# A max-pool-and-subtract kernel: loads and stores in one DMA queue in a fixed order, 4 MB tiles, no ScalarE

## The chip, the cores and the metric

The kernel runs on one core of one Trainium2 chip. The metric is the device time of one execution in microseconds. The profile's "span" runs from the first to the last of the program's own instructions and is 1.5 to 2.3 us shorter than the time. Executions of a kernel are timed several times; those called "fast" are within 1.5% of the fastest of the same kernel. A result counts as faster or slower only beyond 2%; a smaller difference is still told from noise by its 95% interval. Data move between memory and the core in DMAs; 16 DMA engines share each of them, and every engine takes its share as a row of packets. VectorE, ScalarE and GpSimd compute; SyncE and ScalarE issue DMAs here. In the views of the profile these engines are DVE, ACT, POOL and SP, with a q added where the engine only waits or issues.

## The reference

The input is 8 x 64 images of 256 x 256 float32. Each 8 x 8 window's maximum is subtracted from all 64 elements of the window.

```python
x_r = x.reshape(B, C, oH, pH, oW, pW)            # pH = pW = 8
pooled = x_r.max(axis=(3, 5))
upsampled = np.repeat(np.repeat(pooled, pH, axis=2), pW, axis=3)
return (x - upsampled).astype(np.float32)
```

134.2 MB come in and 134.2 MB go out. Eight image lines, 2048 floats or 8 KB, hold 32 whole windows; this is "a row" below. A tile holds R rows per partition, contiguous in memory for a partition.

## The kernel before

Two rows per partition make a tile of 2 MB, 64 tiles in all, in eight buffers. SyncE issues the loads and ScalarE the stores, so there are two DMA queues. A scheduler orders the instructions.

```python
R = 2
data_pool = ctx.enter_context(tc.tile_pool(name="data_pool", bufs=8))
...
for i in range(ntiles):
    dat = data_pool.tile([P, R, row_len], mybir.dt.float32, name="dat")
    nc.sync.dma_start(out=dat..., in_=src)                  # L42, queue 1
    for r in range(R):
        nc.vector.tensor_reduce(out=pooled[:, r], in_=in_v, # L49, max of each window
                                axis=XY, op=max)
    nc.scalar.activation(out=rep, in_=pooled broadcast 8x, func=Copy)   # L56
    for r in range(R):
        nc.vector.tensor_tensor(out=dat_v, in0=dat_v,       # L64
                                in1=rep[:, r] broadcast over 8 lines, op=subtract)
    nc.scalar.dma_start(out=dst, in_=dat...)                # L74, queue 10
```

(Arguments shortened.)

## Time and profile before

| | before |
|---|---|
| time, median | 631.79 us (631.71 to 631.91) |
| span of the profiled execution | 630.3 us |
| DMA rate from 100 to 580 us | 431 GB/s |
| VectorE busy | 564.7 us |

Lines of the page: busy time of the engines, then the 40 slices of the span (busy tenths, GB/s of DMA), the DMA queues, the chain that ended last by engine, and the three costly groups of instructions (busy us, mean ns of one, idle time before them and its releaser).

```profile
DVE 564.7 (90%) x256; ACT 39.5 (6%) x65; POOL 0.2 (0%) x4
DMA  9999999999999999999999999999999999999997
GB/s 361 418 433 433 432 431 432 428 431 433 431 428 433 432 432 433 433 431 432 431 429 431 433 432 428 432 432 431 433 433 431 433 429 429 431 433 433 431 405 334
q1 hardware_dynamic: 9216, 134.22, 50.0%
q10 hardware_dynamic: 9216, 134.22, 49.8%
DMA 81%; DVE 16%; issue 1%; DVEq 0%; ACT 0%; SPq 0%; ACTq 0%
L49 DVE TENSOR_REDUCE pooled<-dat 128x32 f32<-128x2048 f32 x128 | 285.0, 2276 | 57.6 <-DMA dat<-in_x_dram 57.6
L64 DVE TENSOR_TENSOR dat<-dat,rep 128x2048 f32<-128x2048 f32 x128 | 283.9, 2282 | 0.8 <-ACT rep L56 0.8
L56 ACT ACTIVATE rep<-pooled 128x512 f32<-128x512 f32 x64 | 38.2, 624 | 578.4 <-DMA dat<-in_x_dram 408.2
```

The DMA engines are the limit: the row of nines is full, and the rate hardly moves. VectorE is not far behind but waits for loads. The slices at both ends are the only ones clearly lower.

Lines of the timeline of the kernel before at its end (start us, duration us, instruction), then its windows view (window, its length, busy us of VectorE, ScalarE and GpSimd, clock, DMA share, GB/s).

```profile
606.80 8.88 DVE L64 TENSOR_TENSOR dat<-dat,rep 128x2048 f32<-128x2048 f32 x4
...
618.64 4.49 DVE L64 TENSOR_TENSOR dat<-dat,rep 128x2048 f32<-128x2048 f32 x2 [0.76 <-ACT rep L56]
623.17 0.34 ACTq L74 DMA_DIRECT2D out_dram<-dat  x1
```

```profile
620.00:622.00 2.00, 2.00 (x2) 0.00 (x0) 0.00 (x0) 1.00 0.92 393
622.00:624.00 2.00, 1.13 (x1) 0.00 (x0) 0.00 (x0) 1.00 0.02 8
624.00:626.00 2.00, 0.00 (x0) 0.00 (x0) 0.00 (x0) 1.00 1.21 508
626.00:628.00 2.00, 0.00 (x0) 0.00 (x0) 0.00 (x0) 1.00 0.96 410
628.00:630.00 2.00, 0.00 (x0) 0.00 (x0) 0.00 (x0) 1.00 0.31 131
```

The queues run dry at the end because the last store waits for VectorE: 8 GB/s from 622 to 624 us, and the store is issued only at 623.17. (The view counts a packet whole in the window in which it starts, so a short window can show more than the steady rate, as the 508 here.)

### The profile page before, as it was taken

Reading aid. Unit: us, or ns where it says so; the run is one execution under the profiler, and the core shown is the slowest. Engines: PE = TensorE matmul, PEld = TensorE weight load, DVE = VectorE, ACT = ScalarE, POOL = GpSimd, SP = SyncE. Lnnn points to the kernel's source line nnn. Section 1 sums busy time; section 2 is a strip of 40 time slices with the busy share of each in tenths; the row PEclk is TensorE's granted clock in tenths of the full one; section 3 lists DMA queues with packets and bytes.
Section 4 is the critical chain, followed back from the end, with each engine's and each line's share of the span. In section 5 each row is a group of like instructions: output and inputs, shape, how many; then the busy total and the mean of one; then the engine's idle time right before and its main releaser. Section 6 shows DMA issues by size and latency. Waiting matters only on the chain.

```text
span 630.3 us, 730 instructions
## 1 busy us (share of the span) xinstructions
DVE 564.7 (90%) x256; ACT 39.5 (6%) x65; POOL 0.2 (0%) x4
## 2 busy tenths in 40 slices
DVE  4999999889889889889889898898998988988985
ACT  1000010010000000000001001001001001001000
POOL 0000000000000000000000000000000000000000
DMA  9999999999999999999999999999999999999997
GB/s 361 418 433 433 432 431 432 428 431 433 431 428 433 432 432 433 433 431 432 431 429 431 433 432 428 432 432 431 433 433 431 433 429 429 431 433 433 431 405 334
DMA packets 18437, 268.48 MB, mean 426 GB/s; under 512 B 2048, under 2 KB 2048, under 8 KB 2048
## 3 DMA queue, kind: packets, MB, share of 16 engines
q1 hardware_dynamic: 9216, 134.22, 50.0%
q10 hardware_dynamic: 9216, 134.22, 49.8%
q14 instruction: 5, 0.04, 0.0%
HBM read 134.22 MB, written 134.22 MB: 426 GB/s over the span
## 4 chain that ended last, share of the span: by engine, by line
DMA 81%; DVE 16%; issue 1%; DVEq 0%; ACT 0%; SPq 0%; ACTq 0%
DMA dat<-in_x_dram 49%; DMA out_dram<-dat 32%; DVE dat L64 9%; DVE pooled L49 7%; DVEq L100 0%; ACT rep L56 0%; SPq L42 0%; ACTq L74 0%; DVEq L64 0%; ACTq L56 0%
## 5 line engine op out<-in xcount | busy, mean ns | idle before, releaser
L49 DVE TENSOR_REDUCE pooled<-dat 128x32 f32<-128x2048 f32 x128 | 285.0, 2276 | 57.6 <-DMA dat<-in_x_dram 57.6
L64 DVE TENSOR_TENSOR dat<-dat,rep 128x2048 f32<-128x2048 f32 x128 | 283.9, 2282 | 0.8 <-ACT rep L56 0.8
L56 ACT ACTIVATE rep<-pooled 128x512 f32<-128x512 f32 x64 | 38.2, 624 | 578.4 <-DMA dat<-in_x_dram 408.2
L56 ACT ACT_TABLE_LOAD x1 | 1.3, 1283 | 0.7 <-PEq L89 0.7
L89 POOL MEMSET const-uint8-127<- 128x1 uint8 x1 | 0.1, 103 | 0.0
L89 POOL MEMSET const-bfloat16-1.0<- 128x1 bf16 x1 | 0.1, 102 | 0.0
L89 POOL MEMSET const-float32-0.0<- 128x1 f32 x1 | 0.1, 99 | 0.2 <-issue 0.2
L89 POOL MEMSET const-float32-1.0<- 128x1 f32 x1 | 0.1, 99 | 0.0
## 6 DMA issues: line engine op xcount, KB each, us to landing
dat<-in_x_dram SPq DMA_DIRECT2D x64, 2048.0 KB, 29.6
out_dram<-dat ACTq DMA_DIRECT2D x64, 2048.0 KB, 19.0
```

What stands on the lines that cost most here:

```text
L49: nc.vector.tensor_reduce(out=pooled[:, r], in_=in_v, axis=mybir.AxisListType.XY, op=mybir.AluOpType.max,)
L56: nc.scalar.activation(out=rep.rearrange("p r (ow pw) -> p (r ow) pw", pw=pW), in_=pooled.rearrange("p r ow -> p (r ow)").to_broadcast([P, ...
L64: nc.vector.tensor_tensor(out=dat_v, in0=dat_v, in1=rep[:, r].unsqueeze(1).to_broadcast([P, pH, W]), op=mybir.AluOpType.subtract,)
L89: nc = _bacc.Bacc("TRN2", target_bir_lowering=False, num_devices=1)
```

## The change

The intent: fewer and larger transfers (32 KB per partition), a fixed order in which a store never stands in front of a load that is needed sooner, small pieces at both ends, and no ScalarE in the computation. Core of the diff, with cuts and comments added:

```diff
-    R = 2
-    data_pool = ctx.enter_context(tc.tile_pool(name="data_pool", bufs=8))
+TILES = [[2, 2]] + [[4]] * 30 + [[2, 1, 1]]      # rows per piece, pieces per tile
+BUFS = 6
+LEAD = 3
...
-        nc.scalar.activation(out=rep..., in_=pooled..., func=Copy)
-            nc.vector.tensor_tensor(..., in1=rep[:, r]..., op=subtract)
+            nc.vector.tensor_reduce(out=tops, in_=all R rows, ...)      # L50
+        for r in range(R):
+            nc.vector.tensor_tensor(                                     # L57
+                out=wins[:, r], in0=wins[:, r],
+                in1=tops[:, r].unsqueeze(1).unsqueeze(3).to_broadcast([P, pH, oW, pW]),
+                op=mybir.AluOpType.subtract)
...
+    ctx.enter_context(tc.manual_schedule())
+    waiting = []
+    def store():
+        dst, part = waiting.pop(0)
+        nc.sync.dma_start(out=dst, in_=part)                             # L69
...
+        for R in pieces:
+            nc.sync.dma_start(out=part, in_=src)                         # L83
+            if len(waiting) == LEAD:
+                store()
+            pool_and_subtract(part, tops, R)
+            waiting.append((dst, part))
+    while waiting:
+        store()
```

After four loads SyncE's queue reads: store, load, store, load, each of 4 MB.

More of the change, by code (lines that the diff above doesn't have):

```diff
@@ L7 @@
 from concourse._compat import with_exitstack
+F32 = mybir.dt.float32
+ROW = 2048
+TILES = [[2, 2]] + [[4]] * 30 + [[2, 1, 1]]
+BUFS = 6
+LEAD = 3
 @with_exitstack
@@ L21, with pool_and_subtract @@
     pH = pW = 8
-    oH, oW = H // pH, W // pW
+    oW = W // pW
     x_rows = x.rearrange("b c (oh ph) w -> (b c oh) (ph w)", ph=pH)
     out_rows = out.rearrange("b c (oh ph) w -> (b c oh) (ph w)", ph=pH)
-    n_rows = x_rows.shape[0]
-    row_len = x_rows.shape[1]
-    R = 2
-    rows_per_tile = P * R
-    ntiles = n_rows // rows_per_tile
-    assert n_rows % rows_per_tile == 0
-    data_pool = ctx.enter_context(tc.tile_pool(name="data_pool", bufs=8))
-    small_pool = ctx.enter_context(tc.tile_pool(name="small_pool", bufs=4))
-    for i in range(ntiles):
-        dat = data_pool.tile([P, R, row_len], mybir.dt.float32, name="dat")
-        src = x_rows[i * rows_per_tile : (i + 1) * rows_per_tile].rearrange(
-            "(p r) d -> p (r d)", r=R
-        )
-        nc.sync.dma_start(out=dat.rearrange("p r d -> p (r d)"), in_=src)
-        pooled = small_pool.tile([P, R, oW], mybir.dt.float32, name="pooled")
-        rep = small_pool.tile([P, R, W], mybir.dt.float32, name="rep")
-        for r in range(R):
-            in_v = dat[:, r].rearrange("p (ph ow pw) -> p ow ph pw", ph=pH, ow=oW, pw=pW)
+    assert sum(map(sum, TILES)) * P == x_rows.shape[0]
+    size = max(map(sum, TILES))
+    data = ctx.enter_context(tc.tile_pool(name="data", bufs=BUFS))
+    small = ctx.enter_context(tc.tile_pool(name="small", bufs=BUFS))
+    def pool_and_subtract(dat, tops, R):
+        wins = dat.rearrange("p (r ph ow pw) -> p r ph ow pw", r=R, ph=pH, ow=oW)
+        tops = tops.rearrange("p (r ow) -> p r ow", r=R)
+        if R == 1:
             nc.vector.tensor_reduce(
-                out=pooled[:, r],
-                in_=in_v,
+                out=tops[:, 0],
+                in_=wins[:, 0].rearrange("p ph ow pw -> p ow ph pw"),
                 axis=mybir.AxisListType.XY,
@@ L54 @@
             )
-        nc.scalar.activation(
-            out=rep.rearrange("p r (ow pw) -> p (r ow) pw", pw=pW),
-            in_=pooled.rearrange("p r ow -> p (r ow)").to_broadcast([P, R * oW, pW]),
-            func=mybir.ActivationFunctionType.Copy,
-        )
+        else:
+            nc.vector.tensor_reduce(
+                out=tops,
+                in_=wins.rearrange("p r ph ow pw -> p r ow ph pw"),
+                axis=mybir.AxisListType.XY,
+                op=mybir.AluOpType.max,
+            )
         for r in range(R):
-            dat_v = dat[:, r].rearrange("p (ph w) -> p ph w", ph=pH)
             nc.vector.tensor_tensor(
-                out=dat_v,
-                in0=dat_v,
-                in1=rep[:, r].unsqueeze(1).to_broadcast([P, pH, W]),
+                out=wins[:, r],
+                in0=wins[:, r],
+                in1=tops[:, r].unsqueeze(1).unsqueeze(3).to_broadcast([P, pH, oW, pW]),
                 op=mybir.AluOpType.subtract,
             )
-        dst = out_rows[i * rows_per_tile : (i + 1) * rows_per_tile].rearrange(
-            "(p r) d -> p (r d)", r=R
-        )
-        nc.scalar.dma_start(out=dst, in_=dat.rearrange("p r d -> p (r d)"))
+    ctx.enter_context(tc.manual_schedule())
[3 more added lines that the diff above has]
+        nc.sync.dma_start(out=dst, in_=part)
+    at = 0
+    for pieces in TILES:
+        dat = data.tile([P, size * ROW], F32, name="dat")
+        pooled = small.tile([P, size * oW], F32, name="pooled")
+        done = 0
+        for R in pieces:
+            src = x_rows[at : at + P * R].rearrange("(p r) d -> p (r d)", r=R)
+            dst = out_rows[at : at + P * R].rearrange("(p r) d -> p (r d)", r=R)
+            part = dat[:, done * ROW : (done + R) * ROW]
+            tops = pooled[:, done * oW : (done + R) * oW]
+            at += P * R
+            done += R
+            nc.sync.dma_start(out=part, in_=src)
[5 more added lines that the diff above has]
+        store()
 _INS = ['x']
```

## The prediction

> **What bounds the kernel now.** The DMA engines. The page's slices show them 90% busy or more in 39 of 40; the windows view gives 431 GB/s from 100 to 580 us, 427 to 433 in pieces of 20 us. VectorE is busy 564.7 of 630.3 us; its one long idle time, 57.6 us, is put down to loads. The chain of waits is 81% DMA. 268.44 MB at 431 GB/s are 622.8 us of the 630.3. The Trainium skill ("DMA: Bandwidth & Descriptors", section "Where 436 GB/s comes from") puts the ceiling of the 16 ports at 435.2 GB/s; the trace agrees, no 20 us stretch is above 433. At 435.2 the bytes take 616.8 us, so hardly more than 1% can be won.
>
> **The 7.5 us outside the steady rate.** Windows view: the first 5 us move 206 GB/s, about 2.6 us lost. A dip when the first store starts (20 to 25 us: 383 GB/s), about 0.5 us. The last two slices run at 405 and 334 GB/s: after the last load landed (604.6 us) VectorE still had two tiles to do, the DMA engines idled near 611 and from about 622 to 624 us, and the last 2 MB store began only at 623.2. That costs about 3 us. Some 1.6 us follow the last byte.
>
> **What the change does.**
> - One queue for both directions should neither gain nor lose: loads alone (5 to 20 us) ran at 433 GB/s, and stores' packets took 611 ns, also at the end where they ran alone.
> - Transfers of 4 MB: half the packets, of 32 KB if each partition's row stays one packet. A 16 KB packet spends 2 to 5 ns beyond its bytes (estimate: 605 to 608 ns per packet and engine at 433 to 431 GB/s, against 602.4 at 435.2). Halving that gives 1 to 3 us.
> - VectorE: one reduction of 8192 elements for four of 2276 ns saves perhaps 0.4 us per tile; the subtraction with the broadcast read directly should stay at 2.28 us per row. About 17.8 us per 4 MB tile against 19.4 us of DMA (8.39 MB at 433). VectorE stays about 88% busy, no limit.
> - ScalarE's 38 us leave; they were off the path.
> - Queue: load i-3 lands about 58 us of transfers before its store's turn; VectorE needs 18. Load i waits for store i-6, with four transfers (39 us) still queued. I find no moment at which the queue runs dry, nor at the end: the last pieces are small, and 4 MB of the tile before stand ahead of their stores. So the tail's 3 us and the dip go.
>
> **Sum.** 2.6 us start + 268.44 MB at 433 GB/s (620.0) + 1.6 us end + 1.5 us (time less span before) = 625.7 us, 1.0% faster. Range 623.0 to 631.0. Faster by over 2%: 0.01 (it would have to beat the ports' ceiling); within 2%: 0.95; slower by over 2%: 0.04.
>
> **What would show it.** Right: 433 to 434 GB/s in every middle window, about 4480 data packets per direction (8192 before; if unchanged, the rate gain falls away), no dip before the last 2 us, VectorE idle about 70 us behind loads, the queue waiting on stores only. Wrong: the queue waiting on VectorE with the DMA engines idle, subtractions longer than 2.3 us, or a dip at each switch between load and store.
>
> **What would make it wrong.** A cost at each of the 64 switches of direction within one queue (0.1 us each would undo the gain), a slower subtraction, or all engines reading, then all writing, the same memory at once.

## The result, and the profile after

The changed kernel took 631.98 us (median of four, 631.45 to 632.68), the kernel before 631.85 us in the same rounds. The ratio is 1.0004, 95% interval 0.999 to 1.0018: no difference. (Ratios in this document are the mean time of one kernel's fast runs over that of the other's of the same rounds, so not quite the ratio of the medians that are quoted.) The predicted gain of 6 us did not come.

Lines of the page of the changed kernel, in the same order as before:

```profile
DVE 562.3 (89%) x163; POOL 0.2 (0%) x4
DMA  9999999999999999999999999999999999999996
GB/s 366 432 412 441 432 430 430 432 428 432 432 429 426 434 432 432 430 432 430 432 432 432 432 432 432 432 432 432 435 432 432 434 437 432 434 432 429 436 427 261
q1 hardware_dynamic: 10080, 268.44, 99.1%
DMA 53%; DVE 36%; another core or an unknown queue 7%; issue 1%; SPq 0%
L50 DVE TENSOR_REDUCE pooled<-dat 128x128 f32<-128x8192 f32 (+1 forms) x33 | 273.7, 8295 | 43.4 <-DMA dat<-in_x_dram 43.4
L57 DVE TENSOR_TENSOR dat<-dat,pooled 128x2048 f32<-128x2048 f32 x128 | 285.0, 2286 | 1.2
```

The changed kernel's windows view at the end (VectorE and GpSimd only are busy engines here):

```profile
620.00:622.00 2.00, 0.00 (x0) 0.00 (x0) 1.00 1.04 442
622.00:624.00 2.00, 0.00 (x0) 0.00 (x0) 1.00 0.75 315
624.00:626.00 2.00, 0.00 (x0) 0.00 (x0) 1.00 0.32 135
626.00:628.00 2.00, 0.00 (x0) 0.00 (x0) 1.00 0.22 94
628.00:630.00 2.00, 0.00 (x0) 0.00 (x0) 1.00 0.03 12
```

This is the reading that matters. VectorE is done, all stores have been issued, and still the rate sinks in steps, 315, 135, 94, 12 GB/s. In the kernel before, the rate fell to 8 and came back: the queues were empty for a moment. Here it never comes back: a few engines still have work, and the others have none.

Two lines look alarming and are not. "Another core or an unknown queue" in the chain is a DMA that was issued more than 50 us before it landed, which the view does not believe; in this kernel the median store lands 50.1 us after its issue. And the queue's waits:

```profile
SPq L69 <- DVE dat L57: 351.8, 35, 17.6
SPq L83 <- DMA out_dram<-dat: 218.5, 22, 11.3
```

SyncE stands for 351.8 us at stores whose tile VectorE has not finished. But a store lands 50 us after its issue, which is about five transfers of 9.7 us; the DMA engines have work in front of it and don't notice. An experiment below shows that.

**Who is late.** The trace also has every DMA's completion signals. The Trainium skill ("DMA: Bandwidth & Descriptors", section "Why a DMA increments its semaphore by 16 and not by 1") says that each engine that works on a DMA, 16 at most, adds one when its own data has landed; this trace agrees, each DMA has 16 signals. All engines carry the same number of bytes (to within 1% by the reconstruction below), so the time between a DMA's first and last signal says how far the slowest engine is behind the fastest. I call it the spread. Taken from the trace of the changed kernel (not an answer of the profile's views), us from the span's start; the column "6th last" is the slowest of the eleven engines that are left without the five latest:

```
DMA              first signal   6th last    last     spread
load,  first          7.89        8.13      8.33      0.45
store, first         37.75       38.19     38.33      0.59
store, 188 us       187.76      188.25    192.53      4.77
store, 304 us       303.90      304.54    309.71      5.81
store, last         623.52      624.79    629.58      6.05
```

Eleven engines stay within 0.7 us of each other for most of the run and within 1.3 us at the end. Five fall behind, by 3.3 to 6.05 us at the end, nearly all of it before 300 us. The eleven are done at 624.8 us; the span ends 0.94 us after the slowest engine.

**Which packets are late.** A packet of 32 KB takes 1213 ns, but 86 of 7680 took over 100 ns longer, 79 of them before 300 us and 17 of these at the first store. In the kernel before, only 6 packets (of 16 KB) did so after 40 us; 47 did earlier, at the first loads and the first store. The packets carry no engine number, but put in a row by start and end they form 16 unbroken chains with the right bytes, to within 1%. By that inference, about 60 of the 91 packets that were over 50 ns late between 40 and 590 us are the last or second last packet of an engine's share of a load: the engine is late with the end of a load when others have turned to the next store.

The account, in us:

| | before | after |
|---|---|---|
| first engine's last signal | 629.3 | 623.5 |
| spread of the last DMA | 0.2 | 6.05 |
| to the span's end | 0.8 | 0.9 |
| span | 630.3 | 630.5 |

The gain came for the fast engines, and the slow ones gave it back. The 0.2 us before needs care: in that kernel too the engines were apart in the middle, by 1.5 us at the load that lands at 96 us and 3.2 us at the one of 601 us. The lag does not show at its end, because the queues ran dry there and all engines began the last store together.

### The profile page after: what moved, and what is told of

It reads as the page before. It is cut to its first block, busy times and chain, and to the rows that moved or that the text cites. A ratio compares the mean times of both kernels' runs of the same rounds, so it can differ in the third digit from the quotient of the medians.

```text
span 630.5 us, 340 instructions
## 1 busy us (share of the span) xinstructions
DVE 562.3 (89%) x163; POOL 0.2 (0%) x4
## 2 busy tenths in 40 slices
DMA packets 10083, 268.46 MB, mean 426 GB/s; under 512 B 1120, under 2 KB 1120, under 8 KB 1120
## 3 DMA queue, kind: packets, MB, share of 16 engines
q1 hardware_dynamic: 10080, 268.44, 99.1%
## 4 chain that ended last, share of the span: by engine, by line
DMA 53%; DVE 36%; another core or an unknown queue 7%; issue 1%; SPq 0%
DMA dat<-in_x_dram 46%; DVE dat L57 18%; DVE pooled L50 18%; DMA out_dram<-dat 7%; DVE pooled L43 0%; SPq L69 0%
## 5 line engine op out<-in xcount | busy, mean ns | idle before, releaser
L50 DVE TENSOR_REDUCE pooled<-dat 128x128 f32<-128x8192 f32 (+1 forms) x33 | 273.7, 8295 | 43.4 <-DMA dat<-in_x_dram 43.4
L57 DVE TENSOR_TENSOR dat<-dat,pooled 128x2048 f32<-128x2048 f32 x128 | 285.0, 2286 | 1.2
L43 DVE TENSOR_REDUCE pooled<-dat 128x32 f32<-128x2048 f32 x2 | 4.6, 2286 | 7.7 <-DMA dat<-in_x_dram 7.7
## 6 DMA issues: line engine op xcount, KB each, us to landing
out_dram<-dat SPq DMA_DIRECT2D x30, 4096.0 KB, 50.1
```

What stands on the lines that cost most here:

```text
L43: nc.vector.tensor_reduce(out=tops[:, 0], in_=wins[:, 0].rearrange("p ph ow pw -> p ow ph pw"), axis=mybir.AxisListType.XY, op=mybir.AluOp ...
L50: nc.vector.tensor_reduce(out=tops, in_=wins.rearrange("p r ph ow pw -> p r ow ph pw"), axis=mybir.AxisListType.XY, op=mybir.AluOpType.max,)
L57: nc.vector.tensor_tensor(out=wins[:, r], in0=wins[:, r], in1=tops[:, r].unsqueeze(1).unsqueeze(3).to_broadcast([P, pH, oW, pW]), op=mybir ...
```

## The experiments

Theory A: the engines change direction together in one queue, some stall there, and the stalls add up on the same few engines; the time is that of the slowest. Rivals: B, the large rows make some engines slow; C, some engines are slow by themselves; D, VectorE's accesses or its lateness; E, stores in step are slow by themselves. Unless said otherwise an edit is against the changed kernel, and the results are correct.

### 1. A second queue for the stores

```diff
-        nc.sync.dma_start(out=dst, in_=part)
+        nc.scalar.dma_start(out=dst, in_=part)
```

> The changed kernel with its stores issued by ScalarE, so in a second queue; sizes, tiles and VectorE's work as they are. In the changed kernel's trace the 16 completion signals of one DMA drift apart from 0.5 us to 6.0 us (11 engines stay within 0.7 us, 5 fall behind), from long packets at the starts of stores, and the last 6 us of the span are those laggards. Theory A (all engines change direction together in one queue, and stall there): with two queues every engine alternates packets, long packets are seen at the first store only, the spread stays under 3 us, time 625 to 629 us. Rival B (32 KB rows or 4 MB transfers make some engines slow): spread still about 6 us, about 632 us. Rival C (some engines are slow by themselves): the same as B.

Measured: 628.35 us (628.16 to 629.87), ratio to the kernel before 0.9949 (0.9934 to 0.9964). Spread of the last DMA 1.80 us; first engine's last signal at 623.49, as in the changed kernel. Its windows at the end:

```profile
622.00:624.00 2.00, 0.00 (x0) 0.00 (x0) 1.00 0.68 287
624.00:626.00 2.00, 0.00 (x0) 0.00 (x0) 1.00 0.02 8
```

The laggards are gone, and 17 of the 19 packets that were over 100 ns late stand near 20 us, at the first store. So neither large rows (B) nor slow engines (C) are enough by themselves to make the lag, and A stands. That the size of the rows has a part in it is not excluded (experiments 5, 7 and 11). This kernel beats both.

### 2. Two loads, then two stores

```diff
-            if len(waiting) == LEAD:
-                store()
+            if len(waiting) > LEAD and i % 2:
+                store(); store()
```

> The changed kernel, one queue, but two loads and then two stores in turn: half as many changes of direction, each phase 19.4 us rather than 9.7. Theory A1 (engines drift apart until their phases no longer collide; the final lag goes with the length of a phase): spread at the end above 8 us, time 634 to 639 us. Rival A2 (each change of direction costs a fixed stall to some engines): spread about 3 us, time about 629 us. Rivals B and C (size of the rows, slow engines): 6 us and 632 us as before.

Measured: 633.63 us (632.29 to 634.59), spread 6.65 us at the end. Neither form of A was met. The spread grew more slowly (2.0 us at 200 us, against 4.9), as fewer changes of direction would have it, and a step of it came as late as 570 us: the limit that A1 speaks of was not seen. The completion signals show where it grows. At the two loads of a pair that land at 178 and 188 us the spread is 1.38 and 2.01 us, at 217 and 226 us 2.05 and 2.79, at 488 and 498 us 4.46 and 5.48; the stores in between and the first load of the next pair add under 0.1 us each time. It grows at the load that stands just before stores, and not at the load before that. How much a change costs, and whether the pace is in proportion to their number, one trace doesn't show.

### 3. Little work for VectorE (wrong result)

```diff
-            pool_and_subtract(part, tops, R)
+            pool_and_subtract(part[:, :ROW], tops[:, :oW], 1)
```

> The changed kernel with VectorE working on the first row of each piece only; the result is wrong on purpose (three rows of four go out as they came). All DMAs and their order are the same. Theory A: VectorE has no part in the drift; spread about 6 us, time 631 to 632.5 us. Rival D (VectorE's accesses, or stores issued late because VectorE is slow, hold the engines up): spread under 2 us, time about 626 us.

Measured: 632.66 us (632.28 to 634.55), a little over the range of theory A, spread 6.50 us. SyncE's waits in this run:

```profile
SPq L83 <- DMA out_dram<-dat: 483.0, 26, 19.8
SPq L69 <- DMA dat<-in_x_dram: 61.0, 8, 13.9
SPq L69 <- DVE dat L57: 40.8, 9, 4.6
```

The wait for VectorE shrank from 351.8 to 40.8 us and nothing got faster. VectorE worked about a quarter as much, the wait for it nearly went, and the drift stayed: D falls.

### 4. All loads, then all stores (wrong result)

VectorE's work is as in experiment 3, and the DMAs are the same in number, size and queue. Only the order differs.

```diff
-            if len(waiting) == LEAD:
-                store()
...
-    while waiting:
-        store()
+    for n, (dst, R) in enumerate(stores):           # after the last load
+        nc.sync.dma_start(out=dst, in_=parts[n % BUFS][:, : R * ROW])
```

> All 134 MB of loads first and then all 134 MB of stores, one queue, the same transfers, VectorE on one row of each piece; the result is wrong on purpose. One change of direction instead of some 64. Theory A: spread under 2 us throughout, at most one burst of long packets, time 625 to 627 us, which is then also the floor of these transfers. Rival C (slow engines) or E (stores of all engines in step are slow by themselves): spread growing in loads (C) or in stores (E), to 6 us or more, about 632 us.

Measured: 627.75 us (627.6 to 627.88), ratio 0.9934 (0.992 to 0.9949), a little over the expected range, with a spread of 1.0 us at 200 us and 1.68 us at the end. Slices of its page:

```profile
GB/s 371 433 435 429 433 433 425 429 431 435 435 433 431 431 434 425 429 429 435 419 444 436 433 435 431 429 435 427 431 433 435 435 433 435 433 435 433 433 435 345
```

Against experiment 3 this is the cleanest pair: same queue, transfers and VectorE work, 6.50 us of spread when loads and stores alternate, 1.68 us when the direction changes once; 78 packets of 32 KB over 100 ns late against 2. (One thing goes with the order: here no load has to wait until a store has emptied its buffer.) Loads alone (20 to 290 us) ran at 432 GB/s and stores alone (335 to 600 us) at 433, so C and E fall. The slice at the change has 419 GB/s, but the next has 444: as packets are counted where they start, that is no dip.

### 5. One queue, transfers of 2 MB

```diff
-TILES = [[2, 2]] + [[4]] * 30 + [[2, 1, 1]]
-BUFS = 6
-LEAD = 3
+TILES = [[2]] * 63 + [[1, 1]]
+BUFS = 12
+LEAD = 6
```

> One queue as in the changed kernel, but transfers of 2 MB (16 KB per partition, 12 tiles, each store six loads behind): twice as many changes of direction, each phase 4.85 us. The packets of 16 KB make the fastest engine's last transfer land at about 625.8 us rather than 623.5 (1024 packets at 607 ns and 128 signals of 9 ns, against the bigger ones). Theory A1 (engines drift until their phases no longer collide, the limit goes with the phase's length, 6.0 of 9.7 us): spread about 3 us, span about 630, time about 631.5. Theory A2 (a fixed stall at each change, no limit that depends on the length): spread of 8 us or more, time 636 or more.

Measured: 631.94 us (631.65 to 632.02), first engine 625.9, spread 3.44 us. A1's three numbers were met, the spread at 3.44 for 3. The spread stood at 3.0 us by 100 us and hardly grew after. With phases half as long it stops at about half the lag (7.31 us on the same chip, experiment 8), although there are twice as many changes. But the packets are half as long too, so this run can't tell whether the length of a phase or that of a packet sets the limit. Experiment 2, which changed the phases alone, did not double the lag. So changes of direction feed the drift; what bounds it is not shown.

### 6. Two queues, transfers of 2 MB

The edits of 1 and 5 together.

> Two queues as in the first experiment, but transfers of 2 MB (16 KB per partition, 12 tiles). Only the size of rows differs from it. If a packet costs the same few ns whatever its size, the first engine ends near 625.8 us rather than 623.5 and the time is 630 to 631 us, 2 us over the 628.35 of the first experiment. If the size of rows is worth nothing: about 628.3 us.

Measured: 630.70 us (630.57 to 630.76), ratio 0.9983 (0.9971 to 0.9996); first engine at 626.1, spread 1.83 us. Against experiment 1 only the row size differs (and the size of transfers and the number of buffers and pieces that go with it): 2.35 us for rows of 32 KB, or 2.1 us by the ratios, as the two ran in different rounds and on different chips. In the traces two 16 KB packets on one engine start 607.1 ns apart, two of 32 KB 1209.5 ns. Two small ones take 4.7 ns more than a large one, so that is what a packet costs beyond its bytes, if the bytes' own time goes with their number. An estimate with the ceiling cited in the prediction agrees: at 435.2 GB/s over 16 engines the bytes alone are 602.4 and 1204.7 ns, which leaves 4.7 and 4.8.

### 7. Two queues, a smaller start

```diff
-TILES = [[2, 2]] + ...
+TILES = [[1, 1, 2]] + ...
```

(with the edit of 1)

> Two queues and 32 KB rows as in the first experiment, the first tile in pieces of one, one and two rows rather than two and two. The one engine that falls back by about 1.3 us there does so where the first store starts. If a smaller and earlier first store does less harm: spread under 1 us, 627 to 628 us. If the burst is the same whenever the first store comes: 628 to 628.6 us, no difference. Either way faster than the kernel before.

Measured: 643.59 to 662.54 us, median 654.99 of six; only 643.59 and 645.95 count as fast, for which the ratio is 1.0206 (1.0189 to 1.0224), by the 2% rule unclear. Both expectations failed. Slices of the fastest execution:

```profile
GB/s 371 422 439 435 421 429 429 425 425 425 423 427 425 421 423 423 423 421 425 425 427 425 427 425 419 431 419 427 431 419 427 409 435 417 427 423 422 428 426 218
```

The loss is everywhere, not at the ends: 424 GB/s from 100 to 580 us against 433 in experiment 1, and 656 of 7680 packets of 32 KB were over 100 ns late, loads about as often as stores (273 and 324 from 60 to 580 us). The first engine's last signal came at 635.8 us, so here all engines lost, and the spread was 5.0 us on top. Theory A does not explain this: there is no alternating queue. A second queue with 32 KB rows can do badly. The one edit against experiment 1 is the small piece at the start, but the two ran on different chips, and the small start with two queues was run on one only; that the start alone decides is not shown. Experiments 9 and 10, on one chip, show that the start has a part in it.

### 8. The changed kernel again

> The changed kernel once more, word for word, to see whether the drift repeats on another execution. Theory A: the fastest engine's last transfer lands at about 623.5 us again, the spread at the end is 5 to 7 us and the time 631 to 633 us. If the drift were an accident of one execution: spread or time clearly otherwise.

Measured: 633.42 us (631.88 to 634.0), ratio 1.0023 (1.001 to 1.0036). First engine 623.39, spread 7.31 us, both time and spread a little over theory A's ranges. The drift is the kernel's own, and its size varies by about a microsecond.

### 9. Experiment 1 again

> The first experiment's kernel (two queues, 32 KB rows, first tile in two and two rows) word for word, in more rounds, because the same kernel with a smaller start took 644 to 663 us. If the two queues' gain is the kernel's own: 628 to 630 us in all executions, spread about 1.8 us at the end. If it was luck of four executions and each start falls out differently: some executions of 640 us or more.

Measured: 628.66 us (628.38 to 629.72, five), ratio 0.9951 (0.9939 to 0.9964). First engine 623.50, spread 3.04 us in the profiled execution, which was the slowest of the five (1.8 was expected). The gain repeats, on another chip: all nine executions of this kernel lie between 628.16 and 629.87 us.

### 10. Two queues, the first tile whole

```diff
-TILES = [[2, 2]] + ...
+TILES = [[4]] + ...
```

(with the edit of 1)

> Two queues, 32 KB rows, the first tile as one load of 4 MB. In the trace with the small start (one, one, two rows) the engines ended their first load within 0.2 us of each other, in the first experiment within 1.1 us. Theory P (two queues go well when the engines are apart by most of a packet when stores begin, and badly when they are in step): the larger start leaves them about 1 us apart, time 628 to 631 us, long packets only at the first store. Theory Q (what matters is how far the loads are ahead of the stores in steady state, which any other start changes): the outcome is open, 640 us or more is as likely as 629.

Measured: 632.62 us median; 631.76 to 632.69 in three and 641.87 in one that counts as slow. Ratio 1.0007 (0.9992 to 1.0023). At the first load its engines were 0.73 us apart, about as in experiment 9 (0.70), yet the outcome is 4 us worse, on the same chip. Its first engine's last signal came at 625.8 us, so here too all engines lost. Theory P is not supported. Q is not settled: counted in 32 KB packets per engine, the loads of the median engine run 21 to 24 ahead of the stores in experiments 1 and 9, 25 to 26 in experiment 7 and 25 to 27 here. The two that do worse are further ahead, but the lead doesn't tell 632.6 from 655, and no run varied it alone.

### 11. Two queues, 2 MB, a small start

`TILES = [[1, 1]] + [[2]] * 62 + [[1, 1]]`, otherwise as experiment 6.

> Two queues, transfers of 2 MB (16 KB rows) with a small start: first tile in one and one row. With a first piece of two rows it took 630.7 us. If a small start harms any kernel of two queues: 640 us or more, long packets all the way. If it needs rows of 32 KB: 630 to 631.5 us.

Measured: 630.67 us (630.6 to 630.78). With 16 KB rows the start made no difference.

### 12. One queue, the small start of experiment 7

> The changed kernel (one queue, alternate) with the small start of one, one and two rows, as in the kernel that took 655 us with two queues. Theory A (in one queue the drift grows to a limit set by the length of the phases, whatever the start): spread of 5 to 7.5 us at the end, first engine at about 623.5 us, time 631 to 634 us. If the small start itself keeps engines colliding: 640 us or more here too.

Measured: 631.51 us (630.39 to 632.08), ratio 0.9998 (0.9982 to 1.0013), first engine 623.66, spread 4.14 us. The small start does not do in one queue what it did in two (on another chip). The spread came out a little below the expected range, but the profiled execution is the fastest of the four, by up to 1.7 us, so the limit need not depend on the start.

## Why the prediction was right or wrong

It was wrong: 625.7 us and a range of 623.0 to 631.0 were forecast, and 631.98 us came. That the change would be within 2% was right, but for another reason than the one given: two opposite terms of about 6 us cancelled, and that they did so to 0.04% is chance.

- **The bound was right.** DMA is the limit before and after, and VectorE is not: 2286 ns per subtraction and 8683 ns for a reduction of 8192 elements in the view by form (421 ns less than four of 2276), as expected. ScalarE's work left without a trace in the time.
- **The rows' gain was right.** The page has 10080 packets of which 1120 are signals; the remaining 8960 are 4480 per direction, as predicted. Experiments 1 and 6 put the larger rows at 2.1 to 2.35 us, inside the 1 to 3 us.
- **The tail's gain was right as a mechanism.** The queue no longer runs dry at the end (442 GB/s at 620 to 622 us). The first engine's last packet ended at 623.2 us (its signal came at 623.5); the sum put the end of the stream at 622.6 (2.6 + 620.0).
- **The step that failed is "One queue for both directions should neither gain nor lose".** It was drawn from loads alone and stores alone, which do run at full rate (experiment 4 confirms it), and said nothing of the changes between them. The term of the sum that was missing is the lag of the slowest engine: 6.05 us in this trace, 7.31 in another. It took back the rows' and the tail's gain (the first engine's end, 629.3 before and 623.5 after) almost to the microsecond. Some 1.7 us of it stay even with one change of direction (experiment 4) or with a second queue (1.80, experiment 1), so over 4 us are the alternation's; no version tried reached the forecast 625.7.
- **The prediction named the risk and set it too low.** "A cost at each of the 64 switches of direction within one queue (0.1 us each would undo the gain)" is close to what happened: 6.05 us over some 64 changes is 0.09 us each for the slowest engine on average. But it isn't a fixed cost of each change: the spread was 5.81 us by 304 us and hardly grew after. It was listed as a caveat, with the range's upper end nearly at the kernel before but the middle at no cost. Its signature was foreseen as a dip at each change; the mean rate shows little of it (432 GB/s from 100 to 580 us), because eleven engines stay within 0.7 us of each other for most of the run.
- **"433 to 434 GB/s in every middle window" was wrong as a test.** Twenty-microsecond windows swing between 423 and 441. A step of all 16 engines by one packet of 32 KB is 26 GB/s in such a window, so the swing can be the counting alone. A mean over 16 engines cannot show that one of them is late; the steps at the end of the windows view and the completion signals do.
- **VectorE's idle time behind loads** was 51 us rather than the 70 forecast (43.4 in the group above and 7.7 of the two smallest reductions), with no effect on the time.
- **"The queue waiting on stores only" was wrong, and without effect:** 351.8 us of waits for VectorE cost nothing (experiment 3).

What stays open: what inside the engine or the memory holds a load's last packets when other engines have turned to stores; why the lag stops where it does, and whether the size of the packets has a part in it; and why two queues with 32 KB rows do well with one start (628.4 us), indifferently with another (632.6) and badly with a third (655). No run here told these apart, nor was each start run on the same chip.

## What to carry to other kernels

When a transfer is spread over 16 engines, the kernel ends with the slowest of them: compare the first and the last completion signal of a DMA, in the middle of the run and at the end, before trusting a mean rate. In this kernel long alternating phases of loads and stores in one queue cost 4 to 7 us of lag, a single change of direction or a suitable second queue 1.7 to 3.0 us. The best version tried is the changed kernel with its stores in the second queue, 628.4 to 628.7 us (0.5% faster than before), but other starts did worse (experiments 7 and 10); two queues with 2 MB transfers give 630.7 us with either start tried.

## What the Trainium skill lacked or had wrong

- "DMA: Bandwidth & Descriptors", section "Rules for kernel authors", says that spreading DMAs over issuers doesn't help bandwidth and only saves issue time. Here, stores moved to a second queue, nothing else edited, took 628.35 us against 631.98 (both beside 631.85 to 632.0 of the kernel before); with another start two queues took 643.59 us and more. So the choice of queues does change the time. The rate in the middle hardly moved (432 and 433 GB/s from 100 to 580 us); the gain was in how far the engines were apart.
- No page says that engines drift apart when loads and stores alternate in one queue: 6.50 us of spread at the end (experiment 3) against 1.68 us with one change of direction (experiment 4).
- "DMA: Bandwidth & Descriptors", section "Why small descriptors are slow (HBM only)", gives a fixed overhead of about 3 cycles per packet as a matter of small descriptors. The packets here cost about 4.7 ns beyond their bytes at 16 KB and at 32 KB alike (experiment 6), and halving their number was still worth 2.1 to 2.35 us of 630.
- "HBM Reference", section "Specifications (TRN2)", says that a core streaming alone measures about 425 GB/s. With loads and stores together the kernel before held 431 GB/s and the changed one 432 from 100 to 580 us.
